# Order of the weight units in layer A, the start of phase 0, and when the mixes are written

## Chip, cores and metric

One core of one Trainium2 chip runs the whole kernel in one launch. The metric is device microseconds of that core, from runs of the same program; a median over several runs is given. TensorE (PE), VectorE (DVE), ScalarE (ACT), GpSimd (POOL) and the DMA queues run side by side and meet at semaphores.

## The reference

One inference step of a two-layer decoder trunk for a prompt of 16 + 256 rows and 8 sample rows, model width 2048, branch width 4096. Layer A is RWKV-7 time mixing, layer B sliding-window attention. What matters here is the beginning of layer A:

```python
y = xf * lax.rsqrt(jnp.mean(xf * xf, axis=-1, keepdims=True) + RMS_EPS)   # rmsnorm, times a_norm
prev = jnp.concatenate([shift_prev[:, None, :], xn[:, :-1]], axis=1)
xm = xn[:, :, None, :] + (prev - xn)[:, :, None, :] * mu                  # six mixes of every row
rkvz = jnp.einsum('btpd,pde->btpe', xm[:, :, :4], w_rkvz)                 # r, k, v, z: 2048 -> 4096 each
...
kk = k_h * k_k; kk = kk / jnp.maximum(jnp.sqrt(jnp.sum(kk * kk, axis=-1, keepdims=True)), 1e-12)
...                                                                       # the recurrence over 64 heads
y = group_norm(y) + bonus;  return (y * silu(z)) @ w_out
```

Mixes 4 and 5 go through two small (LoRA) products. All arithmetic is float32 in effect: the kernel splits each float32 operand into a high and a low part and sums three products of them.

## The kernel before

Activations lie transposed: 128 partitions by 16 k-tiles by N = 280 columns (272 prompt rows and 8 sample rows). A **product** makes 256 output columns of a projection, that is two PSUM tiles (its column halves, c = 0 and 1) of 128 x 280, over 16 k-tiles. Its weights come in eight **units** of two k-tiles by 256 columns, 256 KB each. `wunits` loads a unit from DRAM (`raw`), and `split` makes `whi` (a cast on ScalarE) and `wlo` (a subtraction on VectorE); `whi` and `wlo` have five buffers each, `raw` four. `mm3` issues three matmuls, `whi` x high mix (L204), `whi` x low mix (L205), `wlo` x high mix (L206). PSUM has three banks for products (`pm`).

**Phase 0** (`phase0`). x is loaded in four chunks, two by SyncE's queue and two by ScalarE's. Squares are made on ScalarE and VectorE, some are added in pairs on VectorE, and products with a matrix of ones (L321) sum them over the partitions into `ps_ssq`. ScalarE takes the root (L323), VectorE a reciprocal and one Newton step (L324 to L328), giving `rsb`. `raw_part(m, g)` makes mix m of two k-tiles (`mst`); for m = 1 it also normalises x and makes the difference of neighbouring rows (L345 to L361). The k projection comes first: `gemm32` makes its first two products (p0 = 0 and 2) in plain float32 from the unsplit mixes (L236), then `proj` makes p0 = 4 and 6 from split mixes, and after them four products of v, while the mixes of v (2), z (3), r (0) and the two LoRA products (L391) are made between (`mixes`, tied behind earlier weight splits by `behind`). While `self.hold` is set, `split` queues its subtraction on VectorE behind the mix that `hold` names: the third of the eight mixes of k. `part` writes the split mixes of k, v and z (`md`, L374) to DRAM as soon as they are made, high and low part each. `proj` ends each product: a copy out of PSUM (L466), and at once, for k, the sums of squares (`ps_kk`, L472), for v the transposes (`ps_vt`, L476). The order on the engines in this phase is a planner's, from the order of the program and its own costs.

**Layer A proper** (`phase_a`). `drive` runs a hand-written order on TensorE: it steps through `products`, a generator that yields after each **piece** (one unit times one column half, 6 matmuls), and between two pieces it issues what the other streams (`main` with the chunk chain, `preps`, `decodes`, ...) have due at that position. Streams other than the epilogues and `main` are queued behind the weight split before the last one made so far (`self.los[-2]`). A unit's load and split are issued in the order of the program when `products` asks for the unit. Units go in pairs: for a pair (h0, h0 + 1) the pieces are (c0, h0), (c0, h0 + 1), (c1, h0), (c1, h0 + 1):

```python
while len(W) < 4: W.append(next(units))      # before a pair
two, W = W[:2], W[2:]
for c in (0, 1):
    for h, (k0, wh, wl) in zip((h0, h0 + 1), two): ...
```

and after the first piece one more unit is asked for. At h = 7 a half is evacuated (`evacuate`, L728 on ScalarE) and after the second `end` stores it. Where the next product uses another mix, `mix_part` loads one of its eight parts from `md` after each piece of the second half. Layer B (`phase_b2`) has the same order in pairs and is not touched.

## Time and profile before

| | us |
|---|---|
| median of 3 runs | 2202.33 |
| lowest, highest | 2187.71, 2206.90 |
| the profiled execution, its own time | 2193.88 |
| its span, first to last instruction | 2191.9 |
| mean granted TensorE clock | 0.986 |
| PE, DVE, ACT busy | 2108.4, 1710.9, 1275.3 |

Three views of the profile are used. The page gives busy time by engine and in 40 equal slices. The timeline gives instructions in order: start, duration, engine, line, output <- inputs, shape, count, and in brackets the idle time before it and what ended it. Groups and waits give sums: for a wait, who waited for whom, total us, times, longest. One fp32 matmul of the source is two matmul records in the trace. Matmuls are pipelined: a record lasts longer than the distance to the next one, so rates are read from distances of starts.

### The profile page before, as it was taken

How to read it: one execution, taken by the hardware profiler on the slowest of the kernel's cores; microseconds unless marked ns; L12 is line 12 of the kernel's file. 1: busy time of each engine (PE TensorE's matmuls, PEld its weight loads, DVE VectorE, ACT ScalarE, POOL GpSimd, SP SyncE). 2: the span in 40 equal slices, each digit the busy share in tenths (PEclk: the TensorE clock that was granted, in tenths of full speed). 3: DMA queues.
4: the chain of work that ended last, by engine and by line, in shares of the span. 5: the costliest groups of instructions: out<-in, count | busy, mean ns of one | idle time of the engine just before them, and what ended most of it. 6: DMA issues, size and time to landing. Idle time of an engine off the chain costs nothing.

```text
span 2191.9 us, 56040 instructions
## 1 busy us (share of the span) xinstructions
PE 2108.4 (96%) x21528; PEld 2006.2 (92%) x21528; DVE 1710.9 (78%) x4118; ACT 1275.3 (58%) x2914; POOL 86.9 (4%) x100
## 2 busy tenths in 40 slices
PE   6998999999999998999999999999999999999997
PEld 5998999999889887998889989999999999999997
DVE  6866767787777776878888786997888888888885
ACT  2557766576766666766666544565555555554443
POOL 0010000000010000000100000110000000000000
PEclk9999999999999999999999999999999999999999
DMA  7887667757666766776645877767554544577774
GB/s 259 301 300 236 191 208 241 209 176 255 202 178 196 242 216 186 260 213 189 195 141 164 275 238 228 241 209 212 155 157 139 166 143 138 170 210 239 231 225 136
DMA packets 277300, 453.10 MB, mean 207 GB/s; under 512 B 53336, under 2 KB 99096, under 8 KB 276640
## 3 DMA queue, kind: packets, MB, share of 16 engines
q1 hardware_dynamic: 276456, 447.44, 66.0%
q8 instruction: 169, 2.77, 0.5%
q10 hardware_dynamic: 576, 2.08, 0.2%
q14 instruction: 99, 0.81, 0.1%
HBM read 385.10 MB, written 68.44 MB: 207 GB/s over the span
## 4 chain that ended last, share of the span: by engine, by line
PE 65%; DMA 5%; DVE 5%; ACT 2%; issue 2%; POOL 1%; SPq 0%; DVEq 0%; POOLq 0%; ACTq 0%
PE ps_z L204 6%; PE ps_z L205 5%; PE ps_z L206 5%; PE ps_ob L206 3%; PE ps_ob L205 3%; PE ps_ob L204 3%; PE ps_q L206 3%; PE ps_q L204 3%; PE ps_q L205 3%; PE ps_oa L205 2%; PE ps_oa L204 2%; PE ps_oa L206 2%; PE ps_r L204 1%; PE ps_o L204 1%; PE ps_k L204 1%
## 5 line engine op out<-in xcount | busy, mean ns | idle before, releaser
L204 PE MATMUL ps_z<-mhlm,whi_z 128*128 128x280 f32 x512 | 160.4, 313 | 0.0
L206 PE MATMUL ps_z<-mhlm,wlo_z 128*128 128x280 f32 x512 | 151.8, 296 | 0.7 <-DVE wlo_z L183 0.7
L204 PE MATMUL ps_q<-bmh,whi_qb 128*128 128x264 f32 x512 | 150.5, 294 | 1.8 <-ACT whi_qb L181 1.8
L205 PE MATMUL ps_z<-mhlm,whi_z 128*128 128x280 f32 x512 | 151.6, 296 | 0.1
L204 PE MATMUL ps_z<-bmh,whi_zb 128*128 128x264 f32 x512 | 147.5, 288 | 0.0
L206 PE MATMUL ps_q<-bmh,wlo_qb 128*128 128x264 f32 x512 | 146.4, 286 | 0.7 <-DVE wlo_qb L183 0.7
L205 PE MATMUL ps_q<-bml,whi_qb 128*128 128x264 f32 x512 | 146.1, 285 | 0.0
L205 PE MATMUL ps_z<-bml,whi_zb 128*128 128x264 f32 x512 | 145.4, 284 | 0.0
L206 PE MATMUL ps_z<-bmh,wlo_zb 128*128 128x264 f32 x512 | 145.4, 284 | 0.0
L204 PE MATMUL ps_ob<-ghi,whi_ob 128*128 128x264 f32 x512 | 145.2, 284 | 0.0
L206 PE MATMUL ps_ob<-ghi,wlo_ob 128*128 128x264 f32 x512 | 144.8, 285 | 0.0
L205 PE MATMUL ps_ob<-glo,whi_ob 128*128 128x264 f32 x512 | 144.5, 283 | 0.0
L181 ACT CAST whi_ob<-raw_ob 128x512 fp32r<-128x512 f32 x128 | 79.2, 621 | 97.0 <-PE ps_ob L205 78.7
L183 DVE TENSOR_TENSOR wlo_r<-raw_r,whi_r 128x512 fp32r<-128x512 f32 x128 | 87.2, 685 | 57.9 <-ACT whi_r L181 56.0
L181 ACT CAST whi_oa<-raw_oa 128x512 fp32r<-128x512 f32 x128 | 79.0, 620 | 91.3 <-PE ps_oa L205 30.5
L183 DVE TENSOR_TENSOR wlo_v<-raw_v,whi_v 128x512 fp32r<-128x512 f32 x128 | 88.0, 691 | 47.7 <-ACT whi_v L181 46.4
L204 PE MATMUL ps_k<-mhlm,whi_k 128*128 128x280 f32 x384 | 120.2, 313 | 2.1 <-ACT whi_k L181 2.1
L204 PE MATMUL ps_v<-mhlm,whi_v 128*128 128x280 f32 x384 | 120.3, 313 | 0.0
L183 DVE TENSOR_TENSOR wlo_k<-raw_k,whi_k 128x512 fp32r<-128x512 f32 x112 | 75.3, 685 | 53.3 <-ACT whi_k L181 49.9
L183 DVE TENSOR_TENSOR wlo_oa<-raw_oa,whi_oa 128x512 fp32r<-128x512 f32 x128 | 87.2, 688 | 36.7 <-ACT whi_oa L181 34.0
L181 ACT CAST whi_zb<-raw_zb 128x512 fp32r<-128x512 f32 x128 | 78.3, 620 | 62.4 <-PE ps_z L205 42.0
L206 PE MATMUL ps_k<-mhlm,wlo_k 128*128 128x280 f32 x384 | 112.6, 293 | 0.3 <-DVE wlo_k L183 0.2
(463 smaller groups left out, 7699.9 us busy)
## 6 DMA issues: line engine op xcount, KB each, us to landing
raw_k<-a_w_rkvz SPq DMA_DIRECT2D x128, 256.0 KB
raw_v<-a_w_rkvz SPq DMA_DIRECT2D x128, 256.0 KB
raw_r<-a_w_rkvz SPq DMA_DIRECT2D x128, 256.0 KB
raw_z<-a_w_rkvz SPq DMA_DIRECT2D x128, 256.0 KB
raw_oa<-a_w_out SPq DMA_DIRECT2D x128, 256.0 KB
raw_qb<-b_w_qz SPq DMA_DIRECT2D x128, 256.0 KB
raw_zb<-b_w_qz SPq DMA_DIRECT2D x128, 256.0 KB
raw_ob<-b_w_o SPq DMA_DIRECT2D x128, 256.0 KB
```

The costliest lines, as they stand in the source:

```text
L181: self.nc.scalar.copy(hi, src)
L183: return self.nc.vector.tensor_tensor(lo, src, hi.bitcast(F32), op=ALU.subtract)
L204: mm(ps, wh, xh, start=start, stop=False)
L205: mm(ps, wh, xl, start=False, stop=False)
L206: return mm(ps, wl, xh, start=False, stop=stop)
```

## The change

1. *Start.* x comes in five chunks, all on SyncE's queue, after the constant tiles are set. Squares, pairwise adds and products of ones are written in one fixed order on TensorE, VectorE and ScalarE, chunk by chunk; 12 products of ones instead of 10. Five and seven products of constant tiles (`filling`), whose result is not used, stand ahead of and behind them. The root is Ln, then Exp with -0.5 on ScalarE; the reciprocal and Newton step go.
2. *Order after it.* `hold` names the last mix of k instead of the third; casts in `split` are queued behind the root; products of p0 = 4 and 6 are queued on TensorE behind the last product of `gemm32`.
3. *Ends of products.* k's sums of squares (`squares`) and v's transposes (`turn_v`) go to a list, `behind`, from which `gemm` takes one after each two units of a later product.
4. *Writes of the mixes.* k's and v's split mixes are written later, up to three during one product (`keep`), each queued on SyncE behind a weight load. z's mixes are stored unsplit, at half the size, and `mix_part` splits them when it loads them.
5. *Layer A.* The pieces of a product go (h, c0), (h, c1) for h = 0 to 7; a unit is asked for when fewer than four of the units from h - 1 on are there.

```diff
+            if self.behind:                                   # gemm, after each two units
+                with self.tc.issue_after(last.ins):
+                    self.behind.pop(0)()
...
-        chunks = [(0, 5), (5, 10), (10, 14), (14, 16)]
-        for i, (a, b) in enumerate(chunks):
-            (late if i % 2 else dma)(xz[:, a:b], I['xT'][:, a:b])
+        for a, b in ((0, 4), (4, 8), (8, 12), (12, 14), (14, 16)):
+            dma(xz[:, a:b], I['xT'][:, a:b])
...
-        ks = (2, 3, 4, 7, 8, 9, 0, 1, 10, 11)
-        for k in ks:
-            nc.tensor.matmul(pss, ones, sq[:, k], start=k == 2, stop=k == 11)
-        A.activation(rsb, pss, AF.Sqrt, scale=1.0 / D, bias=self.epst)
-        V.tensor_scalar(v, pss, 1.0 / D, EPS, op0=MU, op1=AD)
-        V.reciprocal(rsb, rsb)
-        V.tensor_tensor(t, rsb, rsb, op=MU)
-        V.scalar_tensor_tensor(t, t, -0.5, v, op0=MU, op1=MU)
-        V.scalar_tensor_tensor(rsb, t, 1.5, rsb, op0=AD, op1=MU)
+        with self.pe_order(eng.PE, eng.DVE, eng.Activation):
+            filling(5)
+            asq(0, 2)
+            vsq(2, 4)
+            add(0, 2)
+            summed(0, 1)
...
+            asq(14, 15)
+            vsq(15, 16)
+            summed(14, 15)
+            A.activation(rsb, pss[:, :N], AF.Ln, scale=1.0 / D, bias=self.epst)
+            self.root = A.activation(rsb, rsb, AF.Exp, scale=-0.5).ins
+            filling(7)
...
-            if m == 1 and g == 2:
+            if m == 1 and g == 7:
                 self.mixed = last
...
-            if 0 < m < 4:
-                dma(self.md[m][g], hl.bitcast(F32))
+            if m == 2:
+                xm.append(hl)
...
-                        part(m, g, turn)
+                        dma(self.md[m][g], raw_part(m, g))
...
+        def keep(*gs, m=1):
+            for i, g in enumerate(gs):
+                with self.tc.issue_after(self.raws[2 * i - 7].ins):
+                    dma(self.md[m][g], (xk if m == 1 else xm)[g].bitcast(F32))
...
-            self.proj(1, x(xk), [p0], self.kd)
+            with self.tc.issue_after(self.lead):
+                self.proj(1, x(xk), [p0], self.kd)
             mixes(todo)
+            keep(*((0, 1, 2) if p0 == 4 else (3, 4, 5)))
...
-            for h0 in range(0, 8, 2):
+            for h, c in self.PIECES:                          # (0,0) (0,1) (1,0) (1,1) ...
...
-                while len(W) < 4:
+                while len(W) <= h or sum(k >= h - 1 for k in range(len(W))) < 4 and not over:
...
+        if m == 3:                                            # mix_part
+            whole = t[:, 1].bitcast(F32)
+            self.nc.sync.dma_start(whole, d[h])
+            self.split(t[:, 0], t[:, 1], whole)
```

## The prediction

> **What bounds the kernel now.** I read the page's busy table first, then the start in the timeline, then the stretches, then who waits for whom.

> ```profile
> span 2191.9 us, 56040 instructions
> PE 2108.4 (96%) x21528; PEld 2006.2 (92%) x21528; DVE 1710.9 (78%) x4118; ACT 1275.3 (58%) x2914; POOL 86.9 (4%) x100
> PE   6998999999999998999999999999999999999997
> ```

> TensorE is the bound nearly everywhere; only the first and the last slice (55 us each) are clearly below full. So an edit pays only where it takes out a wait of TensorE or a matmul. The first slice is the stage that most of the diff rewrites; here it is in time:

> ```profile
> 9.76 1.69 DVE L306 TENSOR_TENSOR dx<-xn 128x560 f32<-128x560 f32 x2 [1.52 <-DMA xn<-xT]
> 11.51 7.70 PE L321 MATMUL ps_ssq<-dx,ones 128*128 128x280 f32 x20 [11.51 <-DVE dx L306]
> 19.25 0.49 ACT L323 ACTIVATE rsb<-ps_ssq,epst 128x280 f32<-128x280 f32 x1 [8.46 <-PE ps_ssq L321]
> 20.14 1.89 DVE L325 RECIPROCAL rsb<-rsb 128x280 f32<-128x280 f32 x1
> 23.04 0.45 DVE L328 SCALAR_TENSOR_TENSOR rsb<-mt,rsb 128x280 f32<-128x280 f32 x1
> 25.25 6.71 PE L236 MATMUL ps_k<-mst,raw_k 128*128 128x280 f32 x16 [6.04 <-DVE mst L354]
> 31.93 7.71 PE L236 MATMUL ps_k<-mst,raw_k 128*128 128x280 f32 x32
> ...
> L236 PE MATMUL ps_k<-mst,raw_k x128: 397/399/832, 25.3 to 61.7; 128*128 128x280 f32 x128
> ...
> 20.00:30.00 10.00, 4.75 (x10) 3.53 (x11) 9.51 (x21) 2.98 (x6) 0.00 (x0) 0.69 0.12 41
> ```

> Everything of x has landed by about 10.6 us (the second of the two L306 squares of 9.76 starts there). Then 20 records of the products of ones run from 11.51 to 19.2, the root and its Newton step to 23.5, and the first product of the k projection starts at 25.25. TensorE did nothing for the result before 11.5 and from 19.2 to 25.25. The granted clock was 0.69 over 20 to 30 us, and the first 16 records of L236 took 6.71 us where the next 32 took 7.71: 0.42 against 0.24 us each. The whole of this projection is 128 records, to 61.7 us.

> After it TensorE is gapless until the second stage, and DMA nearly full. Layer A follows, with few waits for weights:

> ```profile
> 60.00:100.00 40.00, 40.00 (x285) 38.32 (x285) 34.69 (x69) 24.79 (x48) 0.00 (x0) 1.00 0.90 309
> 100.00:155.00 55.00, 55.00 (x387) 50.95 (x386) 44.06 (x91) 30.86 (x62) 6.04 (x10) 1.00 0.91 318
> ...
> PE ps_wu L1124 <- ACT X L1158: 7.2, 6, 1.9
> PE ps_wu L1124 <- DVE X L1158: 3.9, 4, 2.0
> PE ps_wu L1139 <- ACT W L1131: 3.4, 2, 3.0
> PE ps_o L204 <- ACT whi_oa L181: 3.1, 1, 3.1
> PE ps_o L206 <- DVE wlo_oa L183: 2.4, 3, 1.7
> PE ps_k L204 <- ACT whi_k L181: 2.1, 1, 2.1
> PE ps_r L206 <- DVE wlo_r L183: 0.9, 1, 0.9
> ```

> The last four rows, waits for weights, sum to 8.5 us over the whole of layer A. That is all that a better order of weight units can take out directly.

> **The change part by part.** *Products of ones ahead of the mixes.* Removed: the reciprocal and its five neighbours on VectorE from 19.25 to 23.49 (23.04 + 0.45). Added: Ln and Exp on ScalarE. Their price stands where layer A's end does the same two:

> ```profile
> 1450.49 1.28 ACT L1375 ACT_TABLE_LOAD   x1
> 1452.04 0.50 ACT L1375 ACTIVATE rb<-ps_sta,epst 128x280 f32<-128x280 f32 x1 [0.26 <-PE ps_sta L1373]
> 1456.33 1.28 ACT L1376 ACT_TABLE_LOAD   x1
> 1457.62 0.44 ACT L1376 ACTIVATE rb<-rb 128x280 f32<-128x280 f32 x1
> ```

> Exp behind Ln had a table load of its own, 1.28 us, though Ln's was just in. So I count Ln 0.50 + load 1.28 + Exp 0.44 = 2.2 us. [...] This case's trace has two loads, 1.28 us each, so the trace decides.

> The 12 products of ones now follow the chunks of x as they land; only the last two (4 records) remain behind the last square. From 10.6 us: the last squares, of one k-tile each, 0.5; 4 records at 0.24 make 1.0; the end of the last and the semaphores some 0.5 (an estimate: a record takes 0.40 us in the row of all 128 where the next may start after 0.24, and two semaphores); Ln to Exp 2.2. That gives 14.8 us for the root. From root to first product it was 25.25 - 23.49 = 1.76 us, so the first product starts at 16.5. The filling products only keep TensorE busy: seven, 14 records, from about 12.1 at 0.24 end at 15.5, before 16.5. If the clock is still half then, they take 14 x 0.42 = 5.9 and end at 18.0, and the first product moves to 18.0. If no load is needed or x lands 1 us sooner, it is 15.2. I take 16.5, the full clock, and keep both ends.

> Then 128 records at 0.236 (31 steps in 7.71 less the last one's 0.40) are 30.2 us, to 46.7. VectorE must keep ahead of it, all mixes coming first:

> ```profile
> 29.36 0.93 DVE L345 SCALAR_TENSOR_TENSOR xn<-xn,par,rsb 128x280 f32<-128x280 f32 x2
> ...
> 32.02 0.93 DVE L345 SCALAR_TENSOR_TENSOR xn<-xn,par,rsb 128x280 f32<-128x280 f32 x2
> ...
> L183 DVE TENSOR_TENSOR mhld<-mst,mhld 128x560 fp32r<-128x560 f32 x16 | 11.5, 735 | 0.7 <-ACT mhld L181 0.7
> L183 DVE TENSOR_TENSOR wlo_k<-raw_k,whi_k 128x512 fp32r<-128x512 f32 x16 | 10.6, 685 | 7.7 <-ACT whi_k L181 7.6
> ...
> L204 PE MATMUL ps_k<-mhld,whi_k 128*128 128x280 f32 x10 | 3.5, 354 | 0.0
> ...
> 40.76 0.29 PE L206 MATMUL ps_k<-mhld,wlo_k 128*128 128x280 f32 x1
> 40.89 0.29 PE L204 MATMUL ps_k<-mhld,whi_k 128*128 128x280 f32 x1
> ```

> A pair of mixes is 32.02 - 29.36 = 2.66 us, TensorE's part of it 16 records or 3.8 us: VectorE gains on it. Eight pairs end at 14.8 + 21.3 = 36, and the held-back subtractions (8 x 0.735, and four weight units at 0.685: 8.6 us) at 45, just inside 46.7. That is the cover of moving the hold from the third pair to the eighth; without it each missing subtraction costs 0.7 us of TensorE. Before, TensorE ran 30 fp32r products of the next projection between (10 each of L204, L205, L206); they now follow, at 40.89 - 40.76 = 0.13 us each: 3.9 us. So the state that before reached at 61.9 (61.7 + 0.24) comes at 46.7 + 3.9 = 50.6: **11.3 us** gained, 9.8 to 12.6 by the two ends above. From there to 155 TensorE has the same work and no gap in either, so the gain lasts.

> *Squares of k and transposes of v put behind the next pair of units; k's and v's mixes written three at a time.* In 60 to 155 us TensorE was busy 40.00 of 40 and 55.00 of 55, so their deferral removes no wait: 0. For DMA stand the writes issued before 60 us:

> ```profile
> md<-mhld SPq DMA_DIRECT2D x8, 560.0 KB
> ```

> All eight of k move into this stretch, +4.5 MB, and z's halve, -2.2 MB: +2.3 MB on the 30 MB that 309 and 318 GB/s make of it, at a share of 0.90 and 0.91. That leaves it just under full, so weights stay covered: 0. If they do not, 2.3 MB at 318 GB/s are 7 us.

> *z's mixes stored whole, split when loaded.* Eight casts and eight subtractions leave a stage that TensorE fills and come back in the product ahead of z, there 8 x 0.66 on ScalarE and 8 x 0.73 on VectorE:

> ```profile
> L181 ACT CAST zhld<-mst x8: 655/660/664, 85.6 to 113.7; 128x560 fp32r<-128x560 f32 x8
> L183 DVE TENSOR_TENSOR zhld<-mst,zhld x8: 721/723/739, 88.3 to 114.9; 128x560 fp32r<-128x560 f32 x8
> ```

> On the path 0 to 5.8 us (all eight subtractions of it); each load halves in exchange, so I take 1.

> *Weight units one by one.* Instruction counts stay. What changes is when a unit must be there and when it is let go. The second unit of a pair was needed one piece (6 products) into the pair, now two pieces; every unit is let go after its second piece. With five buffers, the time from letting go to need rises from 6 or 8 pieces to 8. That takes out some of the 8.5 us: 0 to 8.5, I take 3. Against it stands PSUM: with three banks, the next product's second half takes the bank of this product's first half. The first half's end now lies two pieces ahead of that (12 x 0.13 = 1.5 us when nothing is between), where it was four (3.1). The evacuation:

> ```profile
> L728 ACT COPY st<-ps_z x32: 367/388/396, 927.9 to 1217.7; 128x280 f32<-128x280 f32 x32
> ```

> The copy is 0.39 us, plus what ScalarE has in hand: one cast at 0.62 fits into 1.5, two do not. 56 products, from 0 to 0.25 us each (one in four late by a whole copy and cast): 0 to 14 us; I take 4, nearer the low end, as chain work mostly lies between.

> Sum: -11.3 + 0 + 1 - 3 + 4 = **-9.3 us** against the profiled execution's 2193.9 (span 2191.9 and 2.0 around it), 2184.6. That execution lies 8.5 us under the runs' median of 2202.3; the mean of all four times shown is 2197.7, and -9.3 from there is 2188.4. I give 2188.

> [...] The row first: after TensorE's idle 6.04 us the next 16 records took 0.42 us each at a granted 0.69. [...]

> **The rivals.** *Faster by over 1%:* layer A itself loosens. Side work is queued behind the last weight split but one; that split is now nearer to the present, so chains get their turn sooner. It would need half of the X and W waits (14.5 us, 7 of it), all 8.5 of the weights, and 12.6 at the start: -28, about 2170. For it: these waits are on ScalarE and VectorE, not on data from afar. Against: many different small waits, a few us each.

> *Slower by over 1%:* the request comes late. A unit's load, cast and subtraction are now asked for four pieces ahead of use, where it was five to seven; four bare pieces are 3.1 us. A load alone can take longer:

> ```profile
> 750.07 8.75 DMA raw_k<-a_w_rkvz
> ACT whi_r L181 <- DMA raw_r<-a_w_rkvz: 18.1, 15, 3.1
> ```

> If queue order follows the request, a raw load behind a store that waits for its evacuation is late in each of the 64 products. Decisive is whether lateness passes 0.5 us a product: 64 x 0.55 = 35, less 11, is +24, about 2222. Against it: loads wait for a buffer rather than for the request, and the buffers come free as early or earlier.

> *The start's gain is not had:* x in one queue lands later, or VectorE's held subtractions run past 46.7; then 4 to 6 us are left at the start and the whole is about -2, 2196.

> **How the numbers follow.** One per cent (22 us) is about what a measurement of this kernel can tell from no change; its own runs span 19 us. Chances: forecast 0.36, start's gain not had 0.10 (together within 1%: 0.46), faster 0.32, slower 0.22. The likeliest case's own range is 2177 to 2215 (the ends of its terms summed, -21 to +17). The range for all reaches past the faster rival's 2170 by some run spread, to 2162, and into the slower one, to 2219.

> **What would show it.** Right: the first L236 record at 15 to 18 us, its last at 45 to 48, a second table load before Exp, no PE wait for `mst`, the first r products some 11 us sooner. Wrong: PE rows in layer A waiting for `st` copies (PSUM) or for `whi`/`wlo` with more than 20 us in sum; L236 still interleaved; the gain at 155 us under 6. The forecast falls if the span moves by more than 22 us.

## The result, and the profile after

The changed kernel took 2187.53 us (median of 20 runs, 2179.34 to 2201.98) beside 2200.11 us for the kernel before (20 runs): ratio 0.9953, 95% interval 0.9939 to 0.9966. That is 0.5 us from the forecast of 2188, and inside the 1% either way that was given the largest chance. The reasons given for it were mostly wrong, as the runs below show.

One run of all those told of below took far longer than the rest of its kernel (2720 us at a mean clock of 0.69, one of the seven of `after_no_fills`), and its kernel's ratio and clock leave it out.

The profiled execution was the slowest of the 20: 2201.98 us, its span longer than that of the kernel before. A second execution of the same program (`after_again`, span 2187.2) is read beside it where the two differ.

From the page of the changed kernel (span, busy time, PE's 40 slices, a DMA queue of the kind "instruction"):

```profile
span 2200.2 us, 56108 instructions
PE 2122.6 (96%) x21556; PEld 2015.7 (92%) x21556; DVE 1716.4 (78%) x4115; ACT 1272.9 (58%) x2916; POOL 83.4 (4%) x100
PE   9999999999999998999999999999999999999997
...
q8 instruction: 169, 2.77, 0.5%
```

The first slice went from 6 to 9. The start in the timeline (start, duration, engine, line, output <- inputs, count, idle before), one group row, and two stretches (busy time by engine, then granted clock, DMA share, GB/s):

```profile
8.22 4.98 PE L324 MATMUL ps_ssq<-dx,ones 128*128 128x280 f32 x20 [0.29 <-DVE dx L314]
13.04 3.47 PE L320 MATMUL ps_fill<-fill,ones 128*128 128x280 f32 x14
13.24 0.49 ACT L346 ACTIVATE rsb<-ps_ssq,epst 128x280 f32<-128x280 f32 x1 [3.33 <-PE ps_ssq L324]
13.75 1.28 ACT L347 ACT_TABLE_LOAD   x1
15.04 0.44 ACT L347 ACTIVATE rsb<-rsb 128x280 f32<-128x280 f32 x1
17.25 0.97 PE L242 MATMUL ps_k<-mst,raw_k 128*128 128x280 f32 x3 [0.74 <-DVE mst L374]
...
L242 PE MATMUL ps_k<-mst,raw_k x128: 398/399/503, 17.2 to 47.4; 128*128 128x280 f32 x128
...
10.00:20.00 10.00, 9.26 (x40) 7.17 (x39) 4.17 (x11) 4.02 (x7) 0.80 (x3) 1.00 1.04 371
20.00:30.00 10.00, 10.00 (x44) 7.95 (x43) 9.62 (x24) 3.44 (x6) 0.00 (x0) 1.00 0.49 132
50.00:100.00 50.00, 50.00 (x358) 47.55 (x357) 44.33 (x96) 24.06 (x48) 0.00 (x0) 1.00 0.90 309
100.00:145.00 45.00, 45.00 (x321) 42.03 (x320) 31.48 (x58) 23.70 (x51) 5.98 (x10) 1.00 0.93 335
```

The products of ones now run as x lands. Root at 15.5 (15.04 + 0.44), first product at 17.25, last at 47.4, clock 1.00 throughout, and TensorE full from 50 us on. So the stage does what was predicted, 0.7 us late. Layer A begins 10.4 us sooner: the first product of r stands at 153.1 before and at 142.7 after. These are the first and last starts of the first r products (those on phase 0's mixes; the other r products come from 601.5 us on) and of the o products (group rows by tile), before:

```profile
L204 PE MATMUL ps_r<-mhld,whi_r x256: 287/291/495, 153.1 to 287.6; 128*128 128x280 f32 x128
L204 PE MATMUL ps_o<-mhlm,whi_oa x256: 287/291/464, 1214.5 to 1346.8; 128*128 128x280 f32 x128
```

and in the second execution of the changed kernel:

```profile
L207 PE MATMUL ps_r<-mhld,whi_r x256: 287/292/497, 142.5 to 280.6; 128*128 128x280 f32 x128
L207 PE MATMUL ps_o<-mhlm,whi_oa x256: 287/292/403, 1210.6 to 1339.4; 128*128 128x280 f32 x128
```

Of the 10.6 us at 142.5 there are 7.0 left at the last of these r products and 7.4 at the last of o; in the profiled execution the last of o stood at 1353.1, 6 us behind the kernel before. So something in layer A takes the start's gain, and something in it differs from execution to execution. The waits of PE between 150 and 1400 us in that second execution (us in total, times, longest), the rows that bear on the change:

```profile
PE ps_wu L1166 <- DVE X L1200: 5.5, 3, 2.4
PE ps_so L1088 <- issue: 4.9, 4, 2.4
PE ps_k L207 <- ACT whi_k L184: 2.9, 1, 2.9
PE ps_z L208 <- issue: 2.5, 1, 2.5
PE ps_r L207 <- ACT st L770: 2.4, 2, 1.3
PE ps_o L207 <- issue: 2.0, 1, 2.0
PE ps_wu L1166 <- ACT X L1200: 1.9, 3, 0.8
PE ps_v L207 <- ACT st L770: 1.7, 2, 1.3
PE ps_k L209 <- issue: 0.9, 1, 0.9
PE ps_z L207 <- ACT st L770: 0.8, 1, 0.8
```

Three things are to be seen against the rows of before. Waits for weights (`whi`, `wlo`) are down, to 4.3 us in sum from 9.4. Waits for the copies of the sums out of PSUM (`st`, L770) are new. And rows with "issue", a PE that waits for nothing which the profile shows, sum to 10.3 us, where before had one such row:

```profile
PE ps_so L1046 <- issue: 3.4, 3, 1.5
```

### The profile page after: what moved, and what is told of

It reads as the page before. It is cut to its first block, busy times and chain, and to the rows that moved or that the text cites. A ratio compares the mean times of both kernels' runs of the same rounds, so it can differ in the third digit from the quotient of the medians.

```text
span 2200.2 us, 56108 instructions
## 1 busy us (share of the span) xinstructions
PE 2122.6 (96%) x21556; PEld 2015.7 (92%) x21556; DVE 1716.4 (78%) x4115; ACT 1272.9 (58%) x2916; POOL 83.4 (4%) x100
## 3 DMA queue, kind: packets, MB, share of 16 engines
q8 instruction: 169, 2.77, 0.5%
## 4 chain that ended last, share of the span: by engine, by line
PE 82%; DMA 6%; DVE 6%; ACT 4%; issue 2%; SPq 0%; DVEq 0%; POOLq 0%; ACTq 0%
PE ps_z L207 6%; PE ps_z L208 5%; PE ps_z L209 5%; PE ps_ob L209 3%; PE ps_ob L208 3%; PE ps_v L207 3%; PE ps_ob L207 3%; PE ps_q L209 3%; PE ps_q L207 3%; PE ps_q L208 3%; PE ps_k L207 3%; PE ps_v L208 3%; PE ps_v L209 3%; PE ps_k L209 2%; PE ps_k L208 2%; PE ps_r L207 2%
## 5 line engine op out<-in xcount | busy, mean ns | idle before, releaser
L186 DVE TENSOR_TENSOR wlo_z<-raw_z,whi_z 128x512 fp32r<-128x512 f32 x128 | 88.6, 695 | 35.7 <-ACT whi_z L184 32.7
```

What stands on the lines that cost most here:

```text
L186: return self.nc.vector.tensor_tensor(lo, src, hi.bitcast(F32), op=ALU.subtract)
```

## The experiments

The kernels ran in four groups, each beside runs of the kernel before, whose medians were 2199.29, 2199.62, 2201.91 and 2199.61 us; each ratio is to those of its own group. The table puts the runs together. "Position" is the number of TensorE instructions (matmul and weight-load records and its sequencer's) up to layer A's first product, itself included, modulo 256, counted over the trace. The next three columns are sums of PE's waits between 150 and 1400 us in the one profiled execution: those named issue, those for `whi` and `wlo`, those for `st`. The clock is the mean granted one over all the kernel's compared runs. Three of the profiled executions lie far from their kernel's median: that of `phase0_only_aligned` is 9.6 us above it and the slowest of 12, that of `before_spread` 8.8 us above and the slowest of 6, that of `after_last_pair` 10.8 us below and the fastest of 12; their columns are to be read with that. The kernel before's own, 2193.88 us, is 5.4 us below the median in the table. (Two expectations put the waits for weights at about 15 us before, counted against a nominal pitch of the products; the table sums the profile's own rows.)

| kernel | position | issue | weights | copies | clock | us | ratio, 95% |
|---|---|---|---|---|---|---|---|
| before | 122 | 3.4 | 9.4 | 0.0 | 0.985 | 2199.29 | 1 |
| phase0_only | 176 | 10.6 | 8.4 | 0.0 | 0.986 | 2202.63 | 1.0019 (1.0001 to 1.0038) |
| pieces_only | 122 | 5.5 | 2.9 | 7.1 | 0.989 | 2183.99 | 0.9937 (0.9917 to 0.9957) |
| z_split_early | 176 | 6.4 | 5.7 | 4.8 | 0.988 | 2189.43 | 0.9969 (0.9951 to 0.9986) |
| after_again | 176 | 10.3 | 4.3 | 5.1 | 0.988 | 2186.92 | 0.9955 (0.9939 to 0.9971) |
| after_aligned | 120 | 8.6 | 2.6 | 4.1 | 0.989 | 2180.57 | 0.9928 (0.9908 to 0.9948) |
| before_shifted | 178 | 11.5 | 8.7 | 0.0 | 0.984 | 2208.27 | 1.0043 (1.0028 to 1.0059) |
| phase0_only_aligned | 120 | 8.8 | 12.0 | 0.0 | 0.986 | 2199.68 | 1.0008 (0.9990 to 1.0025) |
| pairs_new_requests | 122 | 6.4 | 9.5 | 0.0 | 0.982 | 2205.83 | 1.0023 (1.0005 to 1.0041) |
| before_spread | 122 | 1.5 | 10.7 | 0.6 | 0.980 | 2214.13 | 1.0066 (1.0041 to 1.0091) |
| phase0_only_spread | 176 | 0.8 | 11.1 | 0.0 | 0.981 | 2206.77 | 1.0028 (1.0011 to 1.0045) |
| after_last_pair | 176 | 6.6 | 4.8 | 0.0 | 0.986 | 2193.20 | 0.9959 (0.9941 to 0.9977) |
| after_no_fills | 128 | 4.6 | 2.7 | 8.7 | 0.988 | 2186.31 | 0.9944 (0.9925 to 0.9963) |

### The change taken apart

`phase0_only` is the changed kernel with the old loop over pairs of units in layer A; `pieces_only` is the kernel before with the new loop alone:

```diff
# pieces_only, against the kernel before
+    PIECES = [(h, c) for h in range(8) for c in (0, 1)]
...
-            for h0 in range(0, 8, 2):
+            for h, c in self.PIECES:
...
-                while len(W) < 4:
+                while len(W) <= h or sum(k >= h - 1 for k in range(len(W))) < 4 and not over:
...
# z_split_early, against the changed kernel
...
-                        dma(self.md[m][g], raw_part(m, g))
+                        hl = part(m, g, turn)
+                        dma(self.md[m][g], hl.bitcast(F32))
...
-        if m == 3:                                            # mix_part: z as the other mixes
```

`after_again` is the changed kernel itself.

> All of the change but the order of weight units: layer A keeps pairs of units and the old requests. Theory S (the start carries the whole gain, the order of units is neutral): the stage before layer A ends 10 to 11 us sooner than before and the time is 0.995 of before, as with the whole change. Rival G (the new order gives back inside layer A what the pair of profiled executions shows between 143 and 1224 us, some 16 us): without it the time is 0.988 of before.

> Before, with the new order of weight units in layer A alone. Theory S: 1.000 of before, within 4 us. Rival G: some 16 us slower, 1.007. Rival H (the new order gains and something else gives it back): 0.996 or less.

> The whole change, but z's mixes are split in phase 0 and stored as high and low parts, as before. Theory S: 0.995 of before, 0 to 3 us from the whole change; the stage before layer A has eight subtractions (5.8 us) more on VectorE and is not longer. Rival Z (splitting z's mixes inside layer A is what costs there): the loss between 143 and 1224 us shrinks by 5 us or more, 0.992 or less.

> The changed kernel once more, on the same chip as the three others. Theory S: 0.995 of before; and its profile, another execution, shows the stage before layer A 10 us shorter again, while the loss inside layer A differs by 10 us or more from the first profiled execution's 16, as the runs of one kernel differ by 19 us. Rival G: that loss is 14 to 18 us again.

The parts add up: +0.19% for the start and what hangs on it, -0.63% for the order of units, and -0.45% for both. So the order of units carries the whole gain, and the stage that was to bring 11 us brings none. Neither theory S nor rival G came true: rival H of `pieces_only` did. z's later split may be worth 2.5 us (medians 2186.92 and 2189.43 with it early; the intervals overlap). In its one profile the stage ahead of layer A was longer, which its expectation ruled out: with z's mixes written in both parts, PE waited 2.3 us there for `whi_v`, and layer A's first product came at 145.9 us instead of 142.5.

In `phase0_only` the loss can be followed. Its first r products, and o:

```profile
L207 PE MATMUL ps_r<-mhld,whi_r x256: 287/291/602, 142.7 to 282.2; 128*128 128x280 f32 x128
L207 PE MATMUL ps_o<-mhlm,whi_oa x256: 286/291/582, 1214.5 to 1348.8; 128*128 128x280 f32 x128
```

It is 10.4 us ahead of the kernel before at the first of r, 5.4 at the last of these, level where the o products begin (1214.5 in both) and 2.0 behind at the last of them. That is a loss of 12.4 us over layer A. Against the kernel before, waits named issue are 7.2 us more, all others 1.2 us more, and the windows at half clock in between cost 3.4 us more of full speed (22.2 against 18.8, from the clock records of the two traces): 11.8 of the 12.4. Most of the first five us go at one place. From its timeline of PE, with the products between left out:

```profile
262.08 1.26 PE L1085 MATMUL ps_so<-TN,Noff 32*32 32x16 f32 x128 [1.16 <-DVE TN L1064]
...
266.34 0.29 PE L209 MATMUL ps_r<-mhld,wlo_r 128*128 128x280 f32 x1
268.29 0.29 PE L207 MATMUL ps_r<-mhld,whi_r 128*128 128x280 f32 x1 [1.66 <-issue]
...
268.76 1.21 PE L1091 MATMUL ps_so<-TR,ET 32*16 32x16 f32 x125
272.29 0.23 PE L1091 MATMUL ps_so<-TR,ET 32*16 32x16 f32 x3 [2.32 <-issue]
```

The same stretch in the kernel before:

```profile
271.66 1.26 PE L1040 MATMUL ps_so<-TN,Noff 32*32 32x16 f32 x128 [0.96 <-DVE TN L1019]
...
278.06 1.24 PE L1046 MATMUL ps_so<-TR,ET 32*16 32x16 f32 x128
```

These are the two series of small products in `solve`: 64 fp32 products each, 128 matmul records and 128 weight loads, 256 instructions in 1.2 us. Before, the second went through without a stop. In `phase0_only` PE stops once ahead of it, and once within it, after 125 of 128. Counted over the trace, the two places are 256 instructions apart, and all the stops of over 0.7 us without a wait, in all kernels here, stand at a count of 194 or 195 modulo 256. The queue with the kind "instruction" that suits is q8: 169 packets with 2.77 MB, 16,384 bytes each, for the 2 x 21528 records and some 190 sequencer instructions of the kernel before, which make 168.9 times 256. So by the count a packet goes with a block of 256 instructions. In the stretch of the second stop (DMA by queue: packets, MB, share):

```profile
q8 instruction: 1, 0.02, 5.2%
```

one such packet lies, from 269.70 to 270.78, and PE goes on at 272.29, 1.5 us behind its end. The fourteen traces have 51 stops of over 0.7 us without a wait, and in each of them PE goes on 1.25 to 1.63 us behind the end of such a packet. Ahead of each of the 51, the last 512 instructions had passed in 22 us or less; at 828 other places with the same count they had passed as fast and there was no stop, and at the 1461 where they took longer there was none either. So a dense stretch was there at every stop, but was not enough for one (51 of 879 places). That TensorE waits for instructions there is the author's reading of these counts: nothing in the traces names the wait. The new start has 54 TensorE instructions more than the old (14 more fp32 products at four each, less 2), so layer A's first product stands at 176 modulo 256 instead of 122.

### Does the position in the blocks cost the start its gain?

```diff
# before_shifted (14 products, against the kernel before); after_aligned, phase0_only_aligned (50)
+            for _ in range(50):
+                nc.tensor.matmul(junk[:16, :16], ones[:32, :16], ones[:32, 16:32], start=True, stop=True)
             filling(5)
```

> The kernel before with 14 products of 16 by 16 ahead of its products of ones, while TensorE waits for x: 56 more TensorE instructions and nothing else, so layer A's first product stands at 178 modulo 256, as with the new start (176). Theory F: the stalls without a wait rise from 2 (3.3 us) to about 6 (about 11 us), and the time rises by about 8 us, ratio 1.003 to 1.005. Rival T: ratio 1.000, within 0.001.

> The changed kernel with 50 products of 16 by 16 ahead of the five fills: 200 more TensorE instructions (matmuls and weight loads), written to a bank that nobody reads, at a time when TensorE waits for x. In the profiles so far all stalls of TensorE without a wait lie at instruction counts of 194 to 195 modulo 256, next to one packet of 16384 bytes in the instruction queue. Layer A's first product stands at 122 modulo 256 before and with the unit order alone, and at 176 with the new start, which adds 54 instructions. With 200 more it stands at 120. Theory F (position in the blocks of 256 decides): TensorE's unexplained stalls over 0.7 us in layer A fall from 5 or 6 (10 to 11 us) to 2 to 4 (3 to 5 us), the start's 10 us stay, and the ratio to the kernel before is 0.989 to 0.992. Rival T (the earlier start is lost to something else, such as the chains' waits): stalls shift but the time does not, ratio 0.995 as the changed kernel had.

> The new start with the old order of units, and the 50 products of 16 by 16 ahead of the fills (layer A's first product at 120 modulo 256 instead of 176). Without them its ratio was 1.002. Theory F: stalls without a wait fall from 6 (11.7 us) to about 2 (3 to 4 us), ratio 0.995 to 0.998. Rival T: ratio 1.002 again.

`before_shifted` shows a shift alone: 14 small products in a stretch where TensorE is idle anyway (before, to 11.51 us) cost 0.43%, 9 us, and in its profile the issue waits are 8.1 us more. Its first group of small products stops as that of `phase0_only` did:

```profile
278.90 0.29 PE L206 MATMUL ps_r<-mhld,wlo_r 128*128 128x280 f32 x1 [0.64 <-issue]
...
279.51 1.21 PE L1049 MATMUL ps_so<-TR,ET 32*16 32x16 f32 x124
282.90 0.24 PE L1049 MATMUL ps_so<-TR,ET 32*16 32x16 f32 x4 [2.19 <-issue]
```

`after_aligned` came out at 0.9928, inside the 0.989 to 0.992 expected only with its interval, and below the changed kernel's 0.9955, though the intervals overlap. But its issue waits did not fall to the 3 to 5 us that theory F expected: 8.6 us, against 10.3. So its lead, if it is one, is not shown to come from fewer stops. `phase0_only_aligned` missed: 1.0008, and in its one profile 8.8 us of issue waits instead of 3 to 4, of which one stop at 959.25 us is 4.0:

```profile
PE ps_z L209 <- issue: 4.0, 1, 4.0
```

So a shift alone can cost 9 us, but position 120 doesn't bring back the few stops of the kernel before. Position alone doesn't decide either: `z_split_early` and `after_last_pair` stand at 176 and have 6.4 and 6.6 us, where `phase0_only` and `after_again` at the same position have 10.6 and 10.3. What else decides is not shown; the author's guess is how the series fall in time.

### The stops taken away

```diff
         V.tensor_copy(ET, ps[:, 0:256].rearrange("p (i s) -> p i s", s=16))
-        yield 4
+        yield 16
```

> The kernel before with one number changed: in the solve of a group's triangular blocks, the second run of 64 products of 16 columns (128 records, 256 TensorE instructions in 1.1 us) is due 16 pieces after the first run instead of 4. All the same work is done. Theory F (TensorE waits for its own instructions where two such runs lie within two blocks of 256): the program's pairs of neighbouring blocks with over 330 of their 512 instructions in such runs fall from 20 to 8, so the stalls without a wait (2 of over 0.7 us, 3.3 us, in the profile before) fall to 0 or 1; ratio 0.996 to 1.000, since the chain behind the solve also comes up to 12 pieces (10 us) later in each of 8 groups, at a cost that no profile shows. Rival C (the chain's later end is what counts): ratio 1.002 to 1.01, with more waits of ps_wu and ps_sy for X and W.

> The new start with the old order of units, and the same number changed (the second run of the solve due 16 pieces after the first instead of 4). Without it the ratio was 1.002, with 6 stalls without a wait (11.7 us). Theory F: stalls fall to 0 to 2 (under 4 us), and the start's 10 us come through: 0.4 to 0.5% below the kernel before with the same number changed, which runs beside it. Rival T (the start's gain is lost to the chains' waits, not to instruction fetch): within 0.2% of that kernel or above it, though the stalls are gone.

The stops all but went in both (1.5 and 0.8 us). With them gone the new start comes through in part: 2206.77 against 2214.13 us, 7.4 us or 0.33%, where it brought +0.19% with the stops. Expected were 0.4 to 0.5%, and the two intervals just meet, so the size is not settled. The kernels are slower all the same, as the rival of `before_spread` said, since the chain of chunks ends later. Layer A's o products end sooner (last start 1321.9 in `before_spread` against 1346.8), and then TensorE waits for the chain's tail. From that kernel, a stretch and its largest wait between 1300 and 1450 us:

```profile
1350.00:1400.00 50.00, 34.05 (x209) 32.15 (x210) 33.92 (x65) 18.46 (x30) 1.62 (x3) 0.78 0.71 223
...
PE ps_oa L204 <- ACT ghi L181: 15.1, 3, 7.1
```

TensorE is busy 34 of 50 us there, at a clock of 0.78. So with a distance of 16 pieces the chain's later end costs more than the stops did; no distance between 4 and 16 was run.

### Why the order of units pays

```diff
# pairs_new_requests, against pieces_only: the new loop and its requests, the old order
+    PIECES = [(2 * q + j, c) for q in range(4) for c in (0, 1) for j in (0, 1)]
# after_last_pair, against the changed kernel
+    PIECES = [(h, c) for h in range(6) for c in (0, 1)] + [(6, 0), (7, 0), (6, 1), (7, 1)]
```

> The kernel before with the new loop over the units, but its pieces in the old order (both units of a pair in one half, then both in the other). What is left of the edit is the rule by which a unit's load and split are asked for. The whole edit alone had a ratio of 0.9937. Theory O (the order of the pieces carries the gain, since the units are needed at even distances): ratio about 1.000, weight waits as before (about 15 us in layer A by the nominal pitch), no waits for the copies of the sums. Rival R (the time of the request carries it): ratio 0.993 to 0.995 or better, since the wait for the copies (7 to 9 us in the new order) is not there.

> The changed kernel, with the last two units of each product taken as a pair (both in the first half, then both in the second), the other six one by one. The first half's sum is then complete four pieces before the next product's first half may want its bank's neighbour, as in the kernel before, instead of two. Theory E (the wait for the copies of the sums costs what the traces of the new order show, 6 to 9 us in layer A): these waits vanish, ratio 0.991 to 0.993 against 0.9955. Rival W: the waits for weights, 8 to 10 us in the new order against 15 in the old, come back in exchange, or ScalarE's order is late anyway; ratio 0.995 to 0.997.

It is the order: with the new requests and the old order the ratio is 1.0023 (expected about 1.000), and the waits for weights are as before (9.5). The new order with the old requests was not run, so whether it needs the new ones is open. The waits of `pieces_only`, against the rows shown of before:

```profile
PE ps_wu L1123 <- DVE X L1157: 5.5, 3, 2.4
PE ps_v L204 <- ACT st L727: 2.7, 2, 2.3
PE ps_r L204 <- ACT st L727: 2.5, 2, 1.4
PE ps_wu L1123 <- ACT X L1157: 2.2, 3, 0.9
PE ps_k L204 <- ACT whi_k L181: 1.8, 1, 1.8
...
PE ps_z L204 <- ACT st L727: 1.6, 2, 0.8
```

Weights fall from 9.4 to 2.9 and all other waits of the chains from 35.8 to 24.5 us; the copies rise from 0 to 7.1, issue from 3.4 to 5.5. Together -8.6 us. The rest is probably the clock. The mean granted clock over all runs rises from 0.9852 to 0.9892, which in a span of some 2190 us is 0.0040 x 2190 = 8.8 us of full speed; -17 in sum, for 15 measured. That sum joins the waits of one execution each with the clock of all runs. In the two profiled executions alone the windows at half clock cost 31.0 and 23.8 us of full speed, and -8.6 and -7.2 stand against spans that differ by only 10.3 us (2191.9 and 2181.6). So direction and rough size fit, and the split between waits and clock is not shown closer than that. The clock depends on such waits, as three pairs of neighbouring windows of the kernel before show:

```profile
945.50:948.90 3.40, 1.92 (x134) 1.77 (x122) 2.56 (x7) 0.86 (x3) 0.00 (x0) 1.00 0.80 248
948.90:952.30 3.40, 3.40 (x17) 3.36 (x16) 2.89 (x6) 2.47 (x7) 0.00 (x0) 0.50 0.45 155
...
201.40:204.80 3.40, 1.17 (x9) 0.99 (x8) 2.99 (x6) 3.31 (x10) 0.00 (x0) 1.00 1.01 328
204.80:208.20 3.40, 3.40 (x22) 3.14 (x22) 3.10 (x6) 2.59 (x7) 0.00 (x0) 0.50 0.62 174
...
853.30:856.70 3.40, 1.75 (x38) 1.29 (x36) 3.40 (x8) 3.27 (x11) 0.00 (x0) 1.00 0.54 146
856.70:860.10 3.40, 1.81 (x14) 1.58 (x12) 3.37 (x9) 3.40 (x11) 0.00 (x0) 1.00 0.34 95
```

A window of 3.4 us in which PE was busy 1.17 us is followed by one at 0.50, with 22 matmul records where 3.4 us at the distance of 0.13 us hold 26; 1.75 us busy is followed by a clock of 1.00. A stop of 1.5 us among small products (945.50, busy 1.92) also cost the next window: 17 records. In the third pair 3.2 us of idle time lie in two windows, each just over half busy, and the clock stayed at 1.00, in the window behind them too. Counted over the fourteen traces, in such windows at full clock between 14 and 2150 us: of 121 that were under half busy 113 were followed by one at half, of 50 between 0.50 and 0.55 busy 23, of 198 between 0.55 and 0.75 18, and of 8142 above that none. So by these counts a wait that takes a window under half mostly costs some 1.7 us on top of itself (an estimate: half of 3.41), and the same wait split over two windows often doesn't. Between 14 and 2150 us the stretches at half clock in the traces of the kernel before and the changed one last 3.41 or 6.83 us and begin at multiples of 3.41 us from each other, to within 0.11 us.

`after_last_pair` took the waits for the copies away (0.0), as theory E said, and the time did not follow: 0.9959, not 0.991 to 0.993. Nor did the rival's reason hold, the waits for weights (4.8 against 4.3). Its clock lies 0.0018 above that of the kernel before in its own group, that of `after_again` 0.0027 above, which is some 2 us. What took the place of the 5 us is not shown: the profiled execution, 2182.42 us, is the fastest of its 12, with a median of 2193.20. So taking the waits for the copies away gained nothing that these runs can tell.

### The fills

```diff
-            filling(5)
...
-            filling(7)
```

> The changed kernel without its twelve filling products (five ahead of the products of ones, seven behind). Two things change: TensorE is idle while x and the root are awaited, and there are 48 TensorE instructions fewer, so layer A's first product stands at 128 modulo 256 instead of 176, near the 122 of the kernel before. In its profile the two are apart. Theory K (the fills keep the clock): a half-clock window lies over the first products of the k projection, as in the kernel before, and its last comes at 49 to 51 us instead of 47.35. Rival: the clock is full there anyway, and the last comes at 47 to 48. For the whole: if the position decides (theory F, as with the 50 products of 16 by 16 that gave 0.9928), the stalls without a wait are fewer than 5 and the ratio is 0.993 to 0.995 despite the start; if it does not, the start's loss alone is left and the ratio is 0.996 to 0.998.

Theory K holds. Two stretches of its start, against those of the changed kernel:

```profile
10.00:20.00 10.00, 5.95 (x22) 4.45 (x21) 3.28 (x9) 4.32 (x7) 0.80 (x3) 0.84 1.05 374
20.00:30.00 10.00, 10.00 (x36) 7.74 (x36) 9.58 (x24) 2.90 (x5) 0.00 (x0) 0.82 0.26 84
```

The clock is at half from 16.7 us for two windows, 36 records lie in 20 to 30 us instead of 44, and layer A's first product comes at 146.2 us instead of 142.5 in `after_again`: the fills are worth some 3.6 us at that point. The whole is not slower for it (0.9944 against 0.9955): at position 128 the issue waits are 4.6 instead of 10.3 us, one profile each. This is a sign, beside `before_shifted`, that the new start's 54 instructions cost some of what it gained.

`after_aligned` at 2180.57 us is the fastest of all, 0.9928 (0.9908 to 0.9948); its lead over the changed kernel, which ran in another group, is probable and not settled.

## Why the prediction came out right, step by step

*What bounds the kernel*: right, and left unfinished. TensorE is the bound (busy 96% of the span) and only its waits count. Summing the rows for weights (8.5 us; 9.4 with the two rows for `wlo_z` and `wlo_k` that it left out) as "all that a better order of weight units can take out directly" is right as far as "directly" goes, and missed that a wait can also set the clock of the next 3.4 us (at half after 113 of the 121 windows under half busy).

*The start*: root 14.8 predicted, 15.5 measured; first product 16.5, measured 17.25 (range 15.2 to 18.0); last 46.7, measured 47.4; gain 11.3, measured 10.4 at layer A's first product (range 9.8 to 12.6). Its sign "no PE wait for `mst`" held but for 0.7 us ahead of the first product. The other traces with the old start put that product at 150.9 to 153.2 us, so the gain itself is known to 2 us. Exp had its own table load of 1.28 us, as the trace of before had said (`after` and `after_no_fills`, 1283 ns in both). No run shows the Exp without that load; the early end, 15.2 us, and with it the 12.6 in the faster rival's -28, took it for possible, or x 1 us sooner. x was that much sooner (the last squares began at 9.47 us, not at 10.6), and with the load the first product came at 17.25 all the same. The late end, 18.0 us for the first product with the clock still at half, did not come: with the fills the clock stayed at 1.00.

*"From there to 155 TensorE has the same work and no gap in either, so the gain lasts"*: this step failed. It held to 155 us and was carried to the end of the kernel without following it through layer A. `phase0_only` shows it gone by 1214.5 us. Shown: a shift of 56 TensorE instructions alone costs 9 us with more stops (`before_shifted`), the waits named issue make up 7.2 of the 12.4 us by which `phase0_only` is longer in layer A (one profile each), and 7.4 us of the start come through where the stops are gone. Not settled: that the position is what brings the stops, since both kernels at position 120 kept over 8 us of issue waits, and `phase0_only_aligned` still gained nothing.

*Deferred squares, transposes and writes at 0*: nothing speaks against it. TensorE was busy 50.00 of 50 and 45.00 of 45 us, DMA at 0.90 and 0.93. *z split late at 1* (0 to 5.8): `z_split_early` was not faster, and where it was longer is the stage ahead of layer A, 3.4 us in its profile; the prediction had put the late split's worth there at nothing because TensorE was full, and with z written in both parts it no longer was.

*Units one by one, -3 and +4*: the term that was mis-sized. Measured alone it is -0.63%, some 15 us by the medians. The weights gave -6.5 (within 0 to 8.5) and the copies cost 7.1 (within 0 to 14); not in the sum were 11.3 us of other waits, a rise of 2.1 us in issue waits and 8.8 us of clock. In size it is the layer A part of the rival "layer A itself loosens" (7 and 8.5 us), and the X and W waits of `ps_wu` fell by 6.4, from 15.7 to 9.3, near its 7. Its reason, that side work gets its turn sooner, was not tested.

*Requests too late*: did not happen; waits for weights fell, and the requests alone changed no weight wait. *The start's gain not had*: it was not had, though for another reason than x landing late or subtractions past 46.7.

So the sum was right by luck, because two errors of opposite sign met. The start with all that hangs on it was put at -11.3 + 1 and measured alone at +3.3 us, an error of some 14; the order of units was put at -3 + 4 and measured alone at -15.3, an error of some 16 the other way.

## What to carry to other kernels

Work on a stage that is won early counts only once it has been followed to the end: compare the start of the same products in both traces at several places. Where a stream has hundreds of very small instructions in a row, look for waits named issue and count instructions to them; a few more instructions far ahead moved 9 us here, as much as many an edit brings, so an ablation should be run with a neutral shift beside it. And sum waits by windows of the clock, since a wait of 2 us in one window can cost nearly twice that (2 and 1.7, by the estimate above).
